# Splitting weight blocks four row tiles at a time, with two buffers instead of four

## The chip, the cores and the metric

The kernel runs on one core of one Trainium2 chip. The metric is the device time of one execution in microseconds (us); the figure to compare is the median of several runs. Five engines work side by side, each on its own queue of instructions in a fixed order: PE (TensorE, matrix products), DVE (VectorE), ACT (ScalarE), POOL (GpSimd) and SP, which here only issues DMAs. They wait for each other on semaphores.

## The reference

A decoder trunk of two pre-norm residual layers over 1024 tokens of width 1024, in float32. Each layer is a mixer with an input and an output projection, and a SwiGLU FFN of width 2816:

```
h = x
for layer in range(2):
    hn = rmsnorm(h, mix_norm_g[layer])
    # layer 0: causal pooling + Mamba-2 SSD; layer 1: RWKV-7 + RG-LRU
    h = h + mixer(hn @ w_in) @ w_out
    hn = rmsnorm(h, ffn_norm_g[layer])
    h = h + (silu(hn @ w_gate) * (hn @ w_up)) @ w_down
out = rmsnorm(h, final_norm_g)
```

## The kernel before

The 1024 tokens are worked in two halves of 512 (A and B), one half's mixer scan woven into the other's projections or FFN. A row tile is 128 rows of a weight, the contraction of one product.

To keep float32 accuracy with float32r products, each operand is split into a high half, which is its float32r rounding, and a low half, which is the rest. One product then takes three: high x high, high x low, low x high. Weights are split on chip. `wload` (L321) has SP load a block of four row tiles by 256 columns (512 KB) into one of three `raw` buffers. `wsplit` (L338) takes two row tiles at a time: an ACT cast writes `whi` (L348), then a DVE subtraction writes `wlo` (L349), both 128x512. `whi` and `wlo` each rotate through `BUFS["w"] = 4` buffers of two row tiles, that is two blocks. `dense` (L354) is the loop that uses them; it calls `wblock` for each block and then issues, for each row tile and each of two column tiles, the three products:

```
nc.tensor.matmul(o, wh[:, a:b], xh, start=st, stop=False)      # L370
nc.tensor.matmul(o, wh[:, a:b], xl, start=False, stop=False)   # L371
nc.tensor.matmul(o, wl[:, a:b], xh, start=False, stop=en)      # L372
```

So a block of four row tiles is 24 products of 128x512 on PE. Results are named by stage: `pi` (input projections), `po` (output projection), `pg` and `pu` (gate and up), `py` (down). The FFN goes over groups of column pairs, `GROUPS = (2, 2, 2, 2, 1, 1, 1)`: a group of two pairs has a down projection over four row tiles, a group of one pair over two row tiles, so that its "block" is half a block (L522 adds the result into `h`). The last group's down projection in the second layer (`ffn_final`) has buffers of its own (`alloc`, names `fh` and `fl`). `zload` (L326) loads blocks of 268 columns for z and dt, all eight row tiles of which are kept for four token chunks.

What else is named below: L236 and L302 write the low halves of normed activations, L304 and POOL's L300 the normed values themselves, L613 adds an output projection to the residual, L501 and L510 are the SwiGLU products. L861 makes the SSD's decays. In RWKV, L1166 are the products for the triangular blocks, L1169 masks them into `am`, L1172 and L1173 write `am` to DRAM and L1179 loads parts back in 16 small DMAs. L1040 and L1051 are RG-LRU's exponentials and roots on ACT.

The order of instructions on each engine is not written by hand: the program is emitted as in the loops above, and a scheduler (`schedule_with_timeline_sim=True`) then orders each engine's queue by its own model, and so settles which split, norm or scan instruction stands ahead of which.

Of the kernel before, what the change touches and what calls it, by code (L numbers as in the profile page):

```python
# [13 lines left out]
P = 128  # L14
D = 1024
S = 1024
# [10 lines left out]
BUFS = dict(h=8, m=28, act=5, raw=3, w=4, tf=3, sg=2, st=3, z=6,  # L27
# [64 lines left out]
class Trunk:  # L92
# [48 lines left out]
    def setup_params(self):  # L141
        nc, i = self.nc, self.i
        rows = [self.dp.tile([P, 512], F32, name=f"prow{k}", tag="tf", bufs=BUFS["tf"]) for k in range(2)]
        if NPARAM < 2 * P:
            nc.gpsimd.memset(rows[1], 0.0)
        r = 0
        for n, k in PARAM_ROWS:
            src = i[n]
            while len(src.shape) > 1:
                src = src.rearrange("a b -> (a b)") if len(src.shape) == 2 else src.rearrange("a b c -> (a b c)")  # L150
            src = src.rearrange("(r p) -> r p", p=P)
            done = 0
            while done < k:
                t, o = divmod(r, P)
                m = min(k - done, P - o)
                nc.gpsimd.dma_start(rows[t][o:o + m, :P], src[done:done + m, :])
                r += m
                done += m
        self.par = self.cp.tile([P, NPARAM], F32, name="par")
        ps = self.psum("ps_par")  # L160
        nc.tensor.transpose(ps[:, 0:P], rows[0][:, :P], self.c_ident)
        nc.tensor.transpose(ps[:, P:2 * P], rows[1][:, :P], self.c_ident)
        nc.scalar.copy(self.par, ps[:, :NPARAM])
        # derived parameters
        cw = self.cp.tile([P, 50], F32, name="cw")
        nc.vector.tensor_scalar(cw, self.par[:, PCOL["ssd_conv_w"]:PCOL["ssd_conv_w"] + 50], 0.5, None, op0=MULT)
        self.cw = cw
        omu = self.cp.tile([P, 14], F32, name="omu")
        nc.vector.tensor_scalar(omu, self.pv("rwkv_mu", 0, 14), -1.0, 1.0, op0=MULT, op1=ADD)
        self.omu = omu  # L170
        rkw = self.cp.tile([P, 4, 8], F32, name="rkw")
        nc.vector.tensor_tensor(rkw, self.c_ind.rearrange("p (j h) -> p j h", j=4),
                                self.pv("rwkv_r_k", 0, 4)[:, :, None].to_broadcast([P, 4, 8]), op=MULT)
        self.rkw = rkw
        # SSD per-head vectors on every partition
        hv = self.cp.tile([P, 3, 12], F32, name="hv")
        for k, n in enumerate(("ssd_dt_bias", "ssd_a_log", "ssd_d")):
            nc.gpsimd.dma_start(hv[:, k, :], i[n].broadcast_to([P, 12]))
        self.dtb, self.ssd_d = hv[:, 0, :], hv[:, 2, :]
        na = self.cp.tile([P, 12], F32, name="na")  # L180
        nc.scalar.activation(na, hv[:, 1, :], AF.Exp)
        nc.vector.tensor_scalar(na, na, -1.0, None, op0=MULT)
        self.nega = na
# [5 lines left out]
    def softplus(self, out, x, shape, pool, tag):  # L189
        """out = max(x, 0) + log1p(exp(-|x|)); log1p(u) = 2 atanh(u / (2 + u))."""  # L190
# [26 lines left out]
    def rsqrt1(self, y, x, t):  # L217
        """y = 1 / sqrt(x / 2^26) for [128, 1] operands; the factors that the steps leave cancel exactly."""
        nc = self.nc
        yi, xi = y.bitcast(I32), x.bitcast(I32)  # L220
        nc.vector.tensor_scalar(yi, xi, 1, None, op0=ALU.logical_shift_right)
        nc.vector.tensor_scalar(yi, yi, -1.0, float(0x5F3759DF - 2 ** 31), op0=MULT, op1=ADD)
        for c in (3.0, 12.0, 768.0):
            nc.vector.tensor_scalar(t, y, y, x, op0=MULT, op1=MULT)
            nc.vector.scalar_tensor_tensor(y, t, -c, y, op0=ADD, op1=MULT)

# [11 lines left out]
    def mm3(self, o, w, x, wr=slice(None), wc=slice(None), xr=slice(None)):  # L238
        """o = w^T x from the halves of w and x."""
# [42 lines left out]
    def hload(self, hf, k):  # L282
        """Residual tile k of a half from DRAM."""
        t = self.dp.tile([P, H], F32, name="hraw", tag="st", bufs=BUFS["st"])
        self.nc.sync.dma_start(t, self.hd[hf][k * P:(k + 1) * P, :])
        return t
# [4 lines left out]
    def norm_apply(self, out, h, r, gname, goff, hf=None):  # L291
        """Normalized and split tiles of a half appended to out; yields per tile."""
# [16 lines left out]
    def gain_apply(self, out, h, gname, goff):  # L309
        """Split tiles of h times the gain, whose 1 / rms their products still miss; yields per tile."""  # L310
# [15 lines left out]
    def zload(self, kk):  # L326
        """Rows kk * 128 .. of the first 256 columns of z and the 12 of dt."""
# [6 lines left out]
    def wblock(self, src, nk, width, alloc=None):  # L334
        """src: [nk*128, width] in DRAM -> list of (hi, lo) [128, <=2, width] tiles."""
        return self.wsplit(self.wload(src, nk, width), nk, width, alloc)

    def wsplit(self, raw, nk, width, alloc=None):  # L338
        nc = self.nc
        out = []  # L340
        for k in range(0, nk, 2):
            m = min(2, nk - k)
            if alloc:
                hi, lo = alloc()
            else:
                hi = self.dp.tile([P, 2, WB], F32R, name="whi", tag="whi", bufs=BUFS["w"])
                lo = self.dp.tile([P, 2, WB], F32R, name="wlo", tag="wlo", bufs=BUFS["w"])
# [6 lines left out]
    def dense(self, w, k0, nk, c0, width, rhs, ps, first=True, last=True):  # L354
        """ps[i] (<=128 columns of the weight each) += w[k0*128.., c0:c0+width]^T rhs; yields per block."""
# [25 lines left out]
    def load_x(self, hf, pool, tag, bufs):  # L381
        """x of a half, token-major, scaled by its rstd in place."""
# [24 lines left out]
    def start(self, pool, tag, bufs):  # L407
        """First half of x: norm and split chunk by chunk; the first weights of z run ahead of them."""
# [58 lines left out]
    def x_transposed(self, hf, k, pp):  # L467
        """Tiles k, k + 1 of x^T of a half into two PSUM banks, as the start of their accumulation."""
# [9 lines left out]
    def ffn(self, hf, layer, h, hn, nxt=None, r=None):  # L478
        """h updated in place; yields per weight block; returns Stat of the new h.
        nxt: the tiles that follow hn in its slots, emitted with the last products that read hn.  # L480
        r: 1 / rms per token where hn comes without it."""
# [66 lines left out]
    def ffn_final(self, hf, wd, base, act, h):  # L548
        """Last part of the last down projection, token-major, with the residual and the final norm."""
# [68 lines left out]
    # ================= even layer mixers =================  # L618
# [13 lines left out]
    def conv(self, hf, ps, w, b, car, out):  # L632
        """out = b + sum_k w[k] x[t - 3 + k], x in PSUM; w(k) -> [128, 1]; car: last 3 columns."""
# [10 lines left out]
    def in0(self, hf, hn, st, blk0=None):  # L644
        """Input projection of the even layer with what its columns need at once."""
# [34 lines left out]
    def in0_zdt(self, hf, hn, st, blk=None):  # L680
        """The first 256 columns of z and those of dt, token-major, a chunk after the other."""
# [127 lines left out]
    def ssd(self, hf, st):  # L809
        """SSD over the 4 chunks and 2 groups of a half; yields between steps."""  # L810
# [14 lines left out]
    def ssd_unit(self, hf, st, c, g):  # L825
# [10 lines left out]
        # token-major x and B  # L836
# [10 lines left out]
        # decay[s, h, t] = exp(min(cum_t - cum_s, 0)) for s <= t, for two chunks at a time  # L847
# [47 lines left out]
        # gate with silu(z), group RMS norm  # L895
# [20 lines left out]
    # ================= odd layer mixers =================  # L916
    def odd_open(self, pool):
# [12 lines left out]
        # softplus(-lambda)  # L930
# [13 lines left out]
    def shift(self, hf, ps, f, out):  # L944
        """out = p + mu (prev - p) for the tile f of the RWKV columns."""
# [15 lines left out]
    def in1(self, hf, hn):  # L961
# [24 lines left out]
        # RG-LRU: gate and branch  # L986
# [31 lines left out]
    def lru(self, hf, j2, xcs, ges):  # L1018
# [16 lines left out]
        for t in range(2):  # L1035
            # log_a = lam8 * rg; t = tanh(log_a / 2); 1 / (1 - t) = (1 + exp(log_a)) / 2 refined by one Newton step
# [8 lines left out]
            nc.vector.scalar_tensor_tensor(e, rg, 1.0, y, op0=ADD, op1=MULT)      # a  # L1045
            ys.append(y)
        for t in range(2):
# [4 lines left out]
            nc.vector.scalar_tensor_tensor(y, y, 2.0, rg, op0=MULT, op1=MULT)     # sqrt(1 - a^2)  # L1052
# [8 lines left out]
    def rwkv(self, hf, st):  # L1061
# [9 lines left out]
        # gates of decay and in-context rate  # L1071
# [5 lines left out]
        # squared norms of k * k_k, per head, token on partitions  # L1077
# [30 lines left out]
        # per chunk and head: [z; r] above [A_zk; A_rk]; the part of A that multiplies u  # L1108
# [49 lines left out]
        # inverses of the 32 x 32 diagonal blocks of I - A_zb, one instance per partition  # L1158
# [43 lines left out]
        def prep1(c):  # L1202
            """Token-major k|b and v of a chunk, and its A blocks."""
# [34 lines left out]
        def prep2(c):  # L1238
            """T^T = (I - A_zb)^-T: its diagonal blocks, and the first product of the other one."""
# [21 lines left out]
        def chain1(c):  # L1261
            """[G; Y'] = [z; r] S + [A_zk; A_rk] v"""
# [19 lines left out]
        def chain3(c):  # L1282
            """S <- e^{W_L} (S + [k; b]^T [v; u]), Y = Y' + A_rb u"""
# [48 lines left out]
    def gn(self, hf, c, y, v, bon, gd):  # L1332
        """Group norm, bonus and gate for 128 tokens, in two parts."""
# [49 lines left out]
class Side:  # L1383
    """Work emitted alongside a main stream."""
# [18 lines left out]
def weave(main, side, rate, limit=None):  # L1403
    """Emit main with rate steps of side after each of its steps, for limit steps at most."""
# [12 lines left out]
def hand(main, steps, nxt, side=None, rate=0, counts=(4, 4)):  # L1417
    """Emit main; the tiles nxt, that follow the operand of its last products, with the last two of its steps."""
# [121 lines left out]
```

## Time and profile before

| | us |
|---|---|
| Median of three runs (lowest, highest) | 2456.19 (2454.91, 2458.45) |
| Profiled execution, span from first to last instruction | 2456.8 |
| PE busy in it | 2424.1 |
| DVE, ACT, POOL busy | 1544.5, 915.7, 250.7 |
| `wlo` subtractions on DVE (744) | 539.4 |
| `whi` casts on ACT (744) | 459.2 |

The profiled execution's own time is known only as its span, 2456.8 us. Busy time is the union of an engine's instructions. PEld is the loading of the stationary operand, which overlaps the products. A row of the timeline has the start, the duration, the engine, the line, the operation, out<-in, shapes, a count and in brackets the idle time of the engine before it with what ended it.

### The profile page before, as it was taken

The numbers are of one execution on the slowest core, as the hardware profiler recorded it, in microseconds if no ns is written. First come the engines' busy times: TensorE is split into PE (matmuls) and PEld (weight loads), VectorE is DVE, ScalarE is ACT, GpSimd is POOL, SyncE is SP. The second block draws the span as 40 slices with busy tenths as digits, with TensorE's granted clock in tenths as the row PEclk, the third lists the DMA queues.
The fourth block names the chain that finished last, engine by engine and source line by source line (L and its number), as shares of the span: only waits on it lengthen the run. The fifth ranks groups of instructions, "written<-read, shape, count | busy, mean of one in ns | idle before, by whom it ended". The sixth has DMA issues, their size and how long they took to land.

```text
span 2456.8 us, 33271 instructions
## 1 busy us (share of the span) xinstructions
PE 2424.1 (99%) x12435; PEld 1982.7 (81%) x12435; DVE 1544.5 (63%) x3058; ACT 915.7 (37%) x1612; POOL 250.7 (10%) x235
## 2 busy tenths in 40 slices
PE   7999999999999999999999999999999999999998
PEld 6878888888878887788888888877888888888887
DVE  7888767764476675675565668576565547444445
ACT  4444343322244554233333346432333324222222
POOL 2131121211112010100000111020000001000000
PEclk9999999999999999999999999999999999999999
DMA  5223333233245332543324433234432433333322
GB/s 163 86 88 93 122 98 94 83 111 96 86 138 169 96 105 85 150 144 107 105 79 134 163 120 103 90 108 142 140 97 90 137 125 125 94 95 95 95 94 78
DMA packets 282513, 271.72 MB, mean 111 GB/s; under 512 B 45586, under 2 KB 260776, under 8 KB 282352
## 3 DMA queue, kind: packets, MB, share of 16 engines
q1 hardware_dynamic: 281520, 269.19, 35.4%
q8 instruction: 98, 1.61, 0.3%
q0 software_dynamic: 832, 0.41, 0.1%
q14 instruction: 63, 0.52, 0.1%
HBM read 239.14 MB, written 30.41 MB: 110 GB/s over the span
## 4 chain that ended last, share of the span: by engine, by line
PE 96%; DVE 2%; DMA 1%; issue 0%; ACT 0%; SPq 0%; DVEq 0%; ACTq 0%
PE pu L370 7%; PE pu L371 7%; PE pu L372 7%; PE pg L370 7%; PE pg L371 7%; PE pg L372 7%; PE py L370 6%; PE py L371 6%; PE py L372 6%; PE pi L370 5%; PE pi L372 5%; PE pi L371 5%; PE po L370 2%; PE po L371 2%; PE po L372 2%; PE ps_g L1269 1%
## 5 line engine op out<-in xcount | busy, mean ns | idle before, releaser
L349 DVE TENSOR_TENSOR wlo<-raw,whi 128x512 fp32r<-128x512 f32 (+1 forms) x744 | 539.4, 726 | 537.8 <-ACT whi L348 526.0
L348 ACT CAST whi<-raw 128x512 fp32r<-128x512 f32 (+1 forms) x744 | 459.2, 619 | 1093.3 <-PE pu L371 311.3
L370 PE MATMUL pu<-hnh,whi 128*128 128x512 f32 x736 | 293.9, 399 | 0.0
L371 PE MATMUL pu<-hnl,whi 128*128 128x512 f32 x736 | 292.8, 398 | 0.0
L372 PE MATMUL pu<-hnh,wlo 128*128 128x512 f32 x736 | 291.6, 396 | 0.0
L370 PE MATMUL pg<-hnh,whi 128*128 128x512 f32 x704 | 281.1, 399 | 0.0
L371 PE MATMUL pg<-hnl,whi 128*128 128x512 f32 x704 | 278.7, 396 | 0.0
L372 PE MATMUL pg<-hnh,wlo 128*128 128x512 f32 x704 | 277.2, 395 | 0.0
L371 PE MATMUL py<-actl,whi 128*128 128x512 f32 x672 | 267.2, 398 | 0.0
L370 PE MATMUL py<-acth,whi 128*128 128x512 f32 x672 | 263.6, 402 | 2.3 <-DVE sg L510 1.4
L372 PE MATMUL py<-acth,wlo 128*128 128x512 f32 x672 | 265.0, 396 | 0.0
L370 PE MATMUL pi<-hnh,whi 128*128 128x512 f32 x512 | 204.4, 400 | 1.8 <-DVE xbc L640 1.8
L371 PE MATMUL pi<-hnl,whi 128*128 128x512 f32 x512 | 204.2, 399 | 0.0
L372 PE MATMUL pi<-hnh,wlo 128*128 128x512 f32 x512 | 202.1, 397 | 0.0
L370 PEld LDWEIGHTS pu<-hnh,whi 128*128 128x128 f32 x736 | 138.7, 188 | 33.9 <-issue 2.2
L372 PEld LDWEIGHTS pu<-hnh,wlo 128*128 128x128 f32 x736 | 138.8, 189 | 32.9 <-issue 0.7
L371 PEld LDWEIGHTS pu<-hnl,whi 128*128 128x128 f32 x736 | 138.7, 188 | 32.2 <-issue 0.9
L370 PEld LDWEIGHTS pg<-hnh,whi 128*128 128x128 f32 x704 | 132.4, 188 | 31.1
L372 PEld LDWEIGHTS pg<-hnh,wlo 128*128 128x128 f32 x704 | 132.3, 188 | 30.8
L371 PEld LDWEIGHTS pg<-hnl,whi 128*128 128x128 f32 x704 | 132.3, 188 | 30.4
L370 PEld LDWEIGHTS py<-acth,whi 128*128 128x128 f32 x672 | 127.1, 189 | 34.2 <-ACT hnh L301 1.8
L372 PEld LDWEIGHTS py<-acth,wlo 128*128 128x128 f32 x672 | 127.0, 189 | 29.6
(451 smaller groups left out, 3766.1 us busy)
## 6 DMA issues: line engine op xcount, KB each, us to landing
raw<-in_ffn_w_gate SPq DMA_DIRECT2D x88, 512.0 KB
raw<-in_ffn_w_up SPq DMA_DIRECT2D x88, 512.0 KB
raw<-in_ffn_w_down SPq DMA_DIRECT2D x64, 512.0 KB
raw<-in_od_w_in SPq DMA_DIRECT2D x44, 512.0 KB
raw<-in_ev_w_in SPq DMA_DIRECT2D x36, 512.0 KB
raw<-in_ffn_w_down SPq DMA_DIRECT2D x48, 256.0 KB
yraw<-yd SPq DMA_DIRECT2D x32, 256.0 KB
raw<-in_ev_w_out SPq DMA_DIRECT2D x16, 512.0 KB
```

Of the source, the lines that this page charges most:

```text
L348: nc.scalar.copy(hi[:, :m, :width], raw[:, k:k + m, :width])
L349: nc.vector.tensor_tensor(lo[:, :m, :width], raw[:, k:k + m, :width], hi[:, :m, :width].bitcast(F32), op=SUB)
L370: nc.tensor.matmul(o, wh[:, a:b], xh, start=st, stop=False)
L371: nc.tensor.matmul(o, wh[:, a:b], xl, start=False, stop=False)
L372: nc.tensor.matmul(o, wl[:, a:b], xh, start=False, stop=en)
L1269: nc.tensor.matmul(pg[:, hs], e["w1"][:, h, :], e["S"][:, hs], start=h == 0, stop=h == 7)
```

## The change

`wsplit` takes four row tiles at a time where it allocates from the common pool, and `whi` and `wlo` have two buffers of four row tiles instead of four of two. The bytes of the buffers and the products stay the same; `ffn_final`'s splits stay at two row tiles. Comments and docstrings were taken out as well, and after `wsplit` the line numbers are one higher (L348 is L349, and so on).

```diff
-BUFS = dict(h=8, m=28, act=5, raw=3, w=4, tf=3, sg=2, st=3, z=6,
+BUFS = dict(h=8, m=28, act=5, raw=3, w=2, tf=3, sg=2, st=3, z=6,
...
     def wsplit(self, raw, nk, width, alloc=None):
         nc = self.nc
         out = []
-        for k in range(0, nk, 2):
-            m = min(2, nk - k)
+        step = 2 if alloc else 4
+        for k in range(0, nk, step):
+            m = min(step, nk - k)
             if alloc:
                 hi, lo = alloc()
             else:
-                hi = self.dp.tile([P, 2, WB], F32R, name="whi", tag="whi", bufs=BUFS["w"])
-                lo = self.dp.tile([P, 2, WB], F32R, name="wlo", tag="wlo", bufs=BUFS["w"])
+                hi = self.dp.tile([P, 4, WB], F32R, name="whi", tag="whi", bufs=BUFS["w"])
+                lo = self.dp.tile([P, 4, WB], F32R, name="wlo", tag="wlo", bufs=BUFS["w"])
             nc.scalar.copy(hi[:, :m, :width], raw[:, k:k + m, :width])
             nc.vector.tensor_tensor(lo[:, :m, :width], raw[:, k:k + m, :width], hi[:, :m, :width].bitcast(F32), op=SUB)
             for q in range(m):
                 out.append((hi[:, q, :], lo[:, q, :]))
```

The scheduler orders the new program anew. Three places show what moves. The first is DVE's queue in the odd layer's output projection of half A, where the norm of half B (`hn`, `hnl`) is emitted between its blocks. Before:

```order
L349 TENSOR_TENSOR wlo<-raw,whi 128x2x256
L236 TENSOR_TENSOR hnl_12619<-hn,hnh_12618 128x512
L304 SCALAR_TENSOR_TENSOR hn<-hraw,par,nrb 128x512
L302 SCALAR_TENSOR_TENSOR hnl_12627<-hn,par,hnh_12626 128x512
L349 TENSOR_TENSOR wlo<-raw,whi 128x2x256
L236 TENSOR_TENSOR hnl_12635<-hn,hnh_12634 128x512
L302 SCALAR_TENSOR_TENSOR hnl_12643<-hn,par,hnh_12642 128x512
L613 TENSOR_TENSOR h<-hraw,po 128x512 x2
L349 TENSOR_TENSOR wlo<-raw,whi 128x2x256 x2
```

After, at the same place:

```order
L350 TENSOR_TENSOR wlo<-raw,whi 128x4x256
L236 TENSOR_TENSOR hnl_11827<-hn,hnh_11826 128x512
L304 SCALAR_TENSOR_TENSOR hn<-hraw,par,nrb 128x512
L302 SCALAR_TENSOR_TENSOR hnl_11835<-hn,par,hnh_11834 128x512
L236 TENSOR_TENSOR hnl_11843<-hn,hnh_11842 128x512
L302 SCALAR_TENSOR_TENSOR hnl_11851<-hn,par,hnh_11850 128x512
L614 TENSOR_TENSOR h<-hraw,po 128x512 x2
L350 TENSOR_TENSOR wlo<-raw,whi 128x4x256
```

The split that stood between two norm operations, the last block's first half, is gone; the whole block is split where its second half was, behind both sums into h.

The second is PE's queue at the start of that same last block, `po` being its two accumulators. Before:

```order
L370 MATMUL po_12741<-yh_12379,whi_12783 128x512
L371 MATMUL po_12741<-yl_12380,whi_12783 128x512
L372 MATMUL po_12741<-yh_12379,wlo_12784 128x512
L370 MATMUL po_12742<-yh_12379,whi_12783 128x512
L371 MATMUL po_12742<-yl_12380,whi_12783 128x512
L372 MATMUL po_12742<-yh_12379,wlo_12784 128x512
```

After:

```order
L371 MATMUL po_11865<-yh_11603,whi_11903 128x512
L372 MATMUL po_11865<-yl_11604,whi_11903 128x512
L371 MATMUL po_11866<-yh_11603,whi_11903 128x512
L372 MATMUL po_11866<-yl_11604,whi_11903 128x512
L373 MATMUL po_11865<-yh_11603,wlo_11904 128x512
L373 MATMUL po_11866<-yh_11603,wlo_11904 128x512
```

The first use of wlo moved from the third product to the fifth.

The third is SP's queue in RWKV, half A, where `am` is written and parts of it loaded back (`A<-amd`), beside the FFN's weight loads. Before:

```order
L1173 DMA amd_8662<-am 64x1024
L1172 DMA w1d_8661<-am 64x1024
L1173 DMA amd_8662<-am 64x1024
L1179 DMA A<-amd_8662 8x32x32 x16
L323 DMA raw<-in_ffn_w_up 128x4x256
L323 DMA raw<-in_ffn_w_down 128x4x256 x4
```

After:

```order
L323 DMA raw<-in_ffn_w_up 128x4x256
L1173 DMA w1d_8101<-am 64x1024
L1174 DMA amd_8102<-am 64x1024
L1173 DMA w1d_8101<-am 64x1024
L1174 DMA amd_8102<-am 64x1024
L1180 DMA A<-amd_8102 8x32x32 x16
L323 DMA raw<-in_ffn_w_down 128x4x256 x4
```

The weight load that followed the 16 small loads now stands ahead of them and of the last writes of am.

## The prediction

> **What bounds the kernel now.** I read the page's totals and its chain first, then what TensorE (PE) waits for. Each row here names engine, busy time and share, or the wait, its total, its count and its longest.
>
> ```profile
> PE 2424.1 (99%) x12435; PEld 1982.7 (81%) x12435; DVE 1544.5 (63%) x3058; ACT 915.7 (37%) x1612; POOL 250.7 (10%) x235
> PE 96%; DVE 2%; DMA 1%; issue 0%; ACT 0%; SPq 0%; DVEq 0%; ACTq 0%
> PE ps_g L422 <- DMA grow<-in_mix_norm_g: 8.2, 1, 8.2
> PE ps_x L443 <- DVE xin L440: 4.6, 1, 4.6
> PE ps_A L1166 <- DVE am L1169: 3.0, 3, 2.2
> PE pi L370 <- DVE xbc L640: 1.8, 1, 1.8
> PE py L370 <- DVE sg L510: 1.4, 1, 1.4
> PE po L370 <- ACT hnh L235: 1.3, 1, 1.3
> PE po L370 <- ACT whi L348: 1.0, 1, 1.0
> PE py L370 <- DVE h L522: 0.8, 2, 0.6
> ```
>
> PE is the chain. After the start, whose two waits (8.2 and 4.6 us) are for inputs and the first norm, it waits 9.3 us in all for DVE and ACT (3.0 + 1.8 + 1.4 + 1.3 + 1.0 + 0.8). The splits cost 744 casts on ACT and 744 subtractions on DVE, but only 1.0 us of PE's waits is charged to them. So the change can win a few us at most; what matters is whether it makes PE wait.
>
> Is PE's 99% real? In the last projection stretch PE is without a gap, and one block's first product follows the last one's at once:
>
> ```profile
> 2060.00:2440.00 380.00, 380.00 (x1732) 311.52 (x1731) 176.74 (x305) 109.92 (x196) 0.00 (x0) 1.00 0.30 95
> 2087.16 0.40 PE L370 MATMUL pu<-hnh,whi 128*128 128x512 f32 x1
> 2092.74 0.39 PE L370 MATMUL pu<-hnh,whi 128*128 128x512 f32 x1
> 2092.71 0.62 ACT L348 CAST whi<-raw 128x512 fp32r<-128x512 f32 x1 [2.16 <-PE pu L371]
> 2093.36 0.69 DVE L349 TENSOR_TENSOR wlo<-raw,whi 128x512 fp32r<-128x512 f32 x1 [2.08 <-ACT whi L348]
> ```
>
> The first row holds window, PE, PEld, DVE, ACT, POOL, clock and DMA. The two matmuls are 24 products apart, one whole block: 5.58 us, 0.2325 each, half a block 2.79. The cast starts as its buffer comes free and the subtraction as the cast ends; cast and subtraction take 2094.05 - 2092.71 = 1.34 us.
> The Trainium skill ("Perfetto Trace Analysis", Identifying the Most-Contended Engine) holds that matmul busy time is no good measure of headroom and the weight-load share is. By it the 82% here (311.52 of 380) would leave a fifth to gain. The trace disagrees for feeding: with no gap between products, sooner operands gain nothing here.
>
> **What a split costs, and its lead.** Whole durations (minimum/median/maximum in ns), and other sizes for the slope:
>
> ```profile
> L348 ACT CAST whi<-raw x744: 602/621/642, 9.0 to 2421.7; 128x512 fp32r<-128x512 f32 x184, 128x536 fp32r<-128x536 f32 x2
> L349 DVE TENSOR_TENSOR wlo<-raw,whi x744: 659/691/1811, 9.6 to 2423.7; 128x512 fp32r<-128x512 f32 x184, 128x536 fp32r<-128x536 f32 x2
> L865 ACT ACTIVATE dec<-dec 128x384 f32<-128x384 f32 x32 | 16.1, 521 | 12.7 <-DVE dec L861 12.6
> L236 DVE TENSOR_TENSOR actl<-sg,acth 128x512 fp32r<-128x512 f32 x88 | 57.3, 683 | 0.1
> L873 DVE TENSOR_TENSOR dec<-dec,ps_cb 128x768 f32<-128x768 f32 x16 | 15.1, 946 | 4.0 <-PE ps_cb L872 4.0
> ```
>
> No 1024-wide split stands in the trace; from these rows I estimate ACT 0.621 + 512 x (0.621 - 0.521)/128 = 1.02 us, DVE 0.691 + 512 x (0.946 - 0.683)/256 = 1.22 us. The bounds are twice the 512 (1.24 and 1.38) and the 512 itself plus nothing, which the slope excludes. Of 744 splits 704 become 352; the 40 of two row tiles (down projections of single pairs) stay. ACT saves 352 x (1.24 - 1.02) = 77 us, DVE 352 x (1.38 - 1.22) = 56 us. Both engines run beside PE, so that alone is worth nothing.
>
> What the change takes is lead. With four half-size buffers, a split may start when the half block four back is read, three half blocks (3 x 2.79 = 8.37 us) before PE needs it: 8.37 - 1.34 = 7.0 us to spare. With two whole buffers it may start when the block two back is read, one block (5.58) before: the chain is 1.02 + 1.22 + 0.05 = 2.29, and 3.3 us remain. **In steady blocks that still costs 0.** For the two-tile splits the buffer ahead covers 2.79 against 1.34; two sums into h of 0.68 (as L236) may stand ahead on DVE: 1.34 + 1.36 = 2.70. That just fits: 0. Raw weights are freed 2.29 instead of 1.34 us after a block is read; a load takes 4.25 us (rows below, 1049.62 to 1053.87) and has 3 x 5.58 us: 0. SP's queue holds other DMAs behind that wait, but it already waits there 306 times:
>
> ```profile
> SPq L323 <- DVE wlo L349: 1354.5, 306, 10.8
> ```
>
> So the price is at places where ACT or DVE answers more than 3.3 us late. **First place: the odd layer's first output projection**, where the norm of the other half shares DVE, and DVE operations stretch to 1.79 us:
>
> ```profile
> 1414.49 1.78 DVE L349 TENSOR_TENSOR wlo<-raw,whi 128x512 fp32r<-128x512 f32 x1
> 1416.19 0.68 DVE L236 TENSOR_TENSOR hnl<-hn,hnh 128x512 fp32r<-128x512 f32 x1
> ...
> 1417.46 1.79 DVE L302 SCALAR_TENSOR_TENSOR hnl<-hn,par,hnh 128x512 fp32r<-128x512 f32 x1
> 1419.17 0.68 DVE L349 TENSOR_TENSOR wlo<-raw,whi 128x512 fp32r<-128x512 f32 x1
> 1422.09 1.27 DVE L613 TENSOR_TENSOR h<-hraw,po 128x512 f32<-128x512 f32 x2
> 1423.28 0.68 DVE L349 TENSOR_TENSOR wlo<-raw,whi 128x512 fp32r<-128x512 f32 x1
> 1421.71 0.39 PE L370 MATMUL po<-yh,whi 128*128 128x512 f32 x1
> ```
>
> The last block's halves are split at 1419.17 and 1423.28, ahead of their uses (1421.71 and 2.79 later). Now the one split stands where the second half stood, behind both h sums, while the first half's 0.6 us leave the queue: it ends at 1423.28 - 0.6 + 1.22 = 1423.9 at the earliest, 1424.1 with what is split sooner ahead of it. PE reads wlo first at 1421.71 + 0.93, since the new order puts four whi products ahead: 1422.64. **+1.4 us** (2.7 if nothing is saved ahead of it; 0 if DVE's queue is shorter there than I sum).
>
> **Second place: RWKV's triangular blocks, twice.** SP issues 16 small loads ahead of the weights:
>
> ```profile
> 1038.08 11.44 SPq L1179 DMA_DIRECT2D A<-amd  x16
> 1049.62 0.41 SPq L323 DMA_DIRECT2D raw<-in_ffn_w_up  x1
> 1053.87 1.14 ACT L348 CAST whi<-raw 128x512 fp32r<-128x512 f32 x2 [3.86 <-DMA raw<-in_ffn_w_up]
> 1055.46 0.39 PE L370 MATMUL pu<-hnh,whi 128*128 128x512 f32 x1
> ```
>
> With the old queue the merged split would end at 1053.87 + 2.29 = 1056.16, against 1055.46 + 0.46: 0.2 late, 0.9 with an activation product (L501, as long as L236) ahead on DVE. In the new order that load stands ahead of the 16, so it comes early; but if its buffer isn't free, the writes of am behind it wait, on which PE waited 3.0 us already. I take **+0.6** for both (0 to 1.8).
>
> **Third place: the even layer's first 330 us**, DVE at 81 to 85%. One split there, its cast done at 99.95, stood 6.0 us in DVE's queue:
>
> ```profile
> 35.00:110.00 75.00, 75.00 (x394) 62.51 (x392) 63.88 (x166) 36.98 (x70) 5.67 (x4) 1.00 0.31 92
> 185.00:275.00 90.00, 90.00 (x569) 79.32 (x568) 73.03 (x191) 37.05 (x71) 12.86 (x15) 0.98 0.30 91
> 99.33 0.62 ACT L348 CAST whi<-raw 128x512 fp32r<-128x512 f32 x1 [2.17 <-PE pz L725]
> 105.96 0.67 DVE L349 TENSOR_TENSOR wlo<-raw,whi 128x512 fp32r<-128x512 f32 x1
> 106.46 0.28 PE L724 MATMUL pz<-wlo,hnh 128*128 128x256 f32 x1
> ```
>
> If it kept that place, the merged one would end 0.53 later, at 107.16, 0.7 after PE's first use at 106.46. I allow three such waits, 2.1 us, an estimate since the new order shuffles DVE here: 0 to 3.5, taken **+1.5**.
>
> **The gain.** Each of the nine waits of 9.3 us follows a DVE or ACT queue; one merged split ahead of it saves 0.16 to 0.2 us: **-1.5**. Its bound is all 9.3.
>
> Sum: 0 + 1.4 + 0.6 + 1.5 - 1.5 = +2.0 us on the profiled 2456.8. That execution stands 0.6 us above the runs' median of 2456.19, and inside their range; on the median the forecast is 2458.2. A change of 0.2% (4.9 us) is about what can be told from none.
>
> **Rivals.**
> - Slower by lost lead: the scheduler's new orders cure nothing. Then the three places cost their upper ends, 2.7 + 1.8 + 3.5 = 8.0, and with 1.5 for each of two more crowded stretches of the odd input projections (ACT loads function tables there) 11 us: 2467. It decides once more than three places are over 1.5 us late. For it: lead falls from 7.0 to 3.3 everywhere. Against: one late block lets DVE catch up, so neighbours don't add.
> - Slower by the clock. Rows:
>
> ```profile
> 194.50:199.00 4.50, 4.50 (x14) 3.57 (x15) 2.53 (x10) 1.04 (x2) 0.83 (x1) 0.62 0.38 115
> 199.00:205.00 6.00, 6.00 (x27) 4.76 (x27) 3.53 (x6) 3.43 (x6) 0.00 (x0) 1.00 0.00 0
> 304.00:308.50 4.50, 4.50 (x13) 3.54 (x13) 1.55 (x5) 1.05 (x2) 0.00 (x0) 0.56 0.19 58
> ```
>
>   In 4.5 us 13 or 14 matmuls run instead of 19, at a granted 0.62 and 0.56: 1.3 us lost each. Five more such stretches on top of my sum give 2458.2 + 6.5 = 2465. The second stretch follows a place with PE waits of 1.0 and 1.3 us, the first follows none, so new waits of about 1 us may or may not call one.
>   The Trainium skill ("TensorE: Matmul & The Clock Gate", What's actually happening) says the clock halves after an idle window of about 3.4 us. By that rule my waits, none over 2.7 us, would call none.
> - Faster: the 133 us off ACT and DVE shorten most of PE's 9.3 us, and the reordered first 330 us lose their half-clock stretches (two, 2.6 us): up to 12, likely 7: 2449. Against: only 1.0 us of the waits is charged to a split.
> - The change does nothing visible (+0 to +1), since steady blocks hold 3.3 us of lead: it lies inside my forecast.
>
> **Chances.** Forecast (within 0.2%) 0.50; lost lead 0.28, clock 0.08, faster 0.14. So faster 0.14, same 0.50, slower 0.36. The likeliest case alone spans 2452 to 2461. The range for 8 in 10 reaches into both others: 2451 (leaving out most of the faster case, some 0.12) to 2470 (leaving out 0.06).
>
> **What would show it.** Casts near 1.02 us and subtractions near 1.22, 392 of each with fh's 8 apart; the same gapless PE from 2060 to 2440; new rows "PE ... <- DVE wlo" in PE's waits at 1417 to 1424 us, near 1056 and 1700, and before 330, each under 3 us. I am wrong if those rows sum to over 6 us, if a steady block waits (chain over 5.58), or if PE's waits for DVE shrink by more than 5.

## The result, and the profile after

| | before | after |
|---|---|---|
| Median of 20 runs each on one chip (lowest, highest), us | 2458.37 (2454.70, 2461.14) | 2461.26 (2458.65, 2462.53) |
| Ratio after to before, 95% interval | | 1.0013 [1.0007, 1.0019] |
| Profiled execution, span, us | 2456.8 | 2459.5 |

The kernel is 0.13% slower, some 3 us, inside the 0.2% that the forecast called no change. The forecast was +2.0 us. It came out near, but partly by luck: the odd layer lost more than I had put, and less time at half clock and two vanished waits in the even layer took most of it back.

Page of the kernel after, the totals and its chain:

```profile
PE 2422.6 (98%) x12435; PEld 1976.6 (80%) x12435; DVE 1502.6 (61%) x2706; ACT 852.8 (35%) x1260; POOL 251.8 (10%) x235
PE 89%; DVE 5%; DMA 2%; ACT 1%; SPq 1%; issue 1%; POOL 0%; DVEq 0%; ACTq 0%; POOLq 0%
```

DVE's busy time fell by 41.9 us and ACT's by 62.9, and the time did not fall: their busy time as such is not what the time is made of. PE's share of the chain went from 96 to 89% and DVE's from 2 to 5. The splits and one steady stretch:

```profile
L349 ACT CAST whi<-raw x392: 614/1048/1091, 8.8 to 2429.1; 128x1024 fp32r<-128x1024 f32 x174, 128x512 fp32r<-128x512 f32 x20, 128x1072 fp32r<-128x1072 f32 x2
L350 DVE TENSOR_TENSOR wlo<-raw,whi x392: 676/1225/2311, 9.9 to 2430.3; 128x1024 fp32r<-128x1024 f32 x174, 128x512 fp32r<-128x512 f32 x20, 128x1072 fp32r<-128x1072 f32 x2
2060.00:2440.00 380.00, 380.00 (x1727) 311.47 (x1726) 172.95 (x244) 100.33 (x137) 0.00 (x0) 1.00 0.34 101
```

A merged cast takes 1.05 us and a merged subtraction 1.23, and PE is as gapless from 2060 to 2440 us as before. What PE waited for (engine, operation, the releaser; sum in us, count, longest):

```profile
PE pi L371 <- DVE xbc L639: 2.4, 1, 2.4
PE py L373 <- DVE wlo L350: 2.0, 4, 0.7
PE ps_A L1167 <- DVE am L1170: 1.9, 2, 1.7
PE pi L371 <- DVE r L950: 1.6, 1, 1.6
PE po L373 <- DVE wlo L350: 1.5, 1, 1.5
PE py L371 <- DVE h L523: 1.3, 2, 1.0
PE pi L373 <- DVE wlo L350: 0.6, 1, 0.6
```

Three rows are new, waits for `wlo` of 4.1 us in all, and so is the wait for `r`. Two are gone: 1.0 for `whi` and 1.3 for `hnh` in the even layer's output projection. These rows do not say at what point the time was lost. For that I took each product by its names and shape, in its order, in both traces, and the median difference of the starts over 25 us. Where "after minus before" changes, time was lost or won:

| From to (us) | stage | difference at its end | change | forecast |
|---|---|---|---|---|
| 0-250 | even layer, input projections | +1.4 | +1.4 | +1.5 |
| 250-350 | its output projection, end of the SSD | -3.3 | -4.7 | -1.5 |
| 350-700 | its FFN, steady blocks | -3.6 | -0.3 | 0 |
| 700-1060 | to the first half's RWKV gates | -2.8 | +0.8 | 0 |
| 1060-1080 | triangular blocks, half A | -0.9 | +1.9 | +0.6 with half B |
| 1080-1415 | | -0.9 | 0 | 0 |
| 1415-1430 | odd layer's output projection | +0.9 | +1.8 | +1.4 |
| 1430-1550 | odd layer's input projections, half B | +3.4 | +2.5 | 0 |
| 1550-1700 | FFN, masks of half B | +1.7 | -1.7 | 0 |
| 1700-1730 | triangular blocks, half B | +3.6 | +1.9 | see half A |
| 1730-2440 | | +2.0 | -1.5 | 0 |

Three of these changes hold a difference of the clock. Before's profile has stretches at half the granted clock at 195, 301 and 1619 us, and the profile after has none there; each step of 3.41 us costs about 1.55 us (last section). Without these four steps the changes to 250, to 350 and to 1700 us would be about +2.9, -1.6 and -0.1, and the new kernel would end some 8 us behind instead of 2. The +0.8 at 700 to 1060 holds a new wait of 1.0 us for `h`, at 717 us.

An operation of known place bears the table out. `ps_kr` runs in RWKV's gates of each half; its first and last start stand behind the durations. Before, then after:

```profile
L1124 PE MATMUL ps_kr<-knT,indt_r x16: 387/392/500, 966.2 to 1617.8; 8*128 8x512 f32 x16
```

```profile
L1125 PE MATMUL ps_kr<-knT,indt_r x16: 384/392/506, 964.3 to 1621.9; 8*128 8x512 f32 x16
```

The new kernel reaches half A's gates 1.9 us earlier and half B's 4.1 us later.

### The profile page after: what moved, and what is told of

It is laid out like the page before. It is cut to its first block, busy times and chain, and to the rows that moved or that the text cites. A ratio compares the mean times of both kernels' runs of the same rounds, so it can differ in the third digit from the quotient of the medians.

```text
span 2459.5 us, 32078 instructions
## 1 busy us (share of the span) xinstructions
PE 2422.6 (98%) x12435; PEld 1976.6 (80%) x12435; DVE 1502.6 (61%) x2706; ACT 852.8 (35%) x1260; POOL 251.8 (10%) x235
## 4 chain that ended last, share of the span: by engine, by line
PE 89%; DVE 5%; DMA 2%; ACT 1%; SPq 1%; issue 1%; POOL 0%; DVEq 0%; ACTq 0%; POOLq 0%
PE pg L372 6%; PE pu L371 6%; PE pg L371 6%; PE pu L372 6%; PE pg L373 6%; PE pu L373 6%; PE py L371 6%; PE py L373 6%; PE py L372 6%; PE pi L371 4%; PE pi L373 4%; PE pi L372 4%; PE po L373 2%; PE po L371 2%; PE po L372 2%; PE ps_g L1270 1%
## 5 line engine op out<-in xcount | busy, mean ns | idle before, releaser
L349 ACT CAST whi<-raw 128x1024 fp32r<-128x1024 f32 (+2 forms) x392 | 393.7, 1004 | 978.8 <-PE pu L372 296.1
L350 DVE TENSOR_TENSOR wlo<-raw,whi 128x1024 fp32r<-128x1024 f32 (+2 forms) x392 | 465.9, 1188 | 322.2 <-ACT whi L349 311.5
L373 PE MATMUL pu<-hnh,wlo 128*128 128x512 f32 x736 | 283.4, 396 | 0.0
L373 PE MATMUL pg<-hnh,wlo 128*128 128x512 f32 x704 | 269.2, 395 | 0.0
L373 PE MATMUL py<-acth,wlo 128*128 128x512 f32 x672 | 253.6, 397 | 2.0 <-DVE wlo L350 2.0
L373 PE MATMUL pi<-hnh,wlo 128*128 128x512 f32 x512 | 196.1, 396 | 0.9 <-DVE wlo L350 0.6
L523 DVE TENSOR_TENSOR h<-h,py 128x512 f32<-128x512 f32 x160 | 108.1, 684 | 82.7 <-PE py L373 82.1
```

Of the source, the lines that this page charges most:

```text
L349: nc.scalar.copy(hi[:, :m, :width], raw[:, k:k + m, :width])
L350: nc.vector.tensor_tensor(lo[:, :m, :width], raw[:, k:k + m, :width], hi[:, :m, :width].bitcast(F32), op=SUB)
L523: nc.vector.tensor_tensor(h[f], h[f], pp[t], op=ADD)
```

## The experiments

Three theories stood against each other. Length: a subtraction of 1.2 us, whole or not at all, is late where DVE is crowded. Buffers: with two whole buffers a split may only start when a whole block has been read, so the lead is lost, whatever the operations' length. Order: each rebuild is ordered anew by the scheduler, and the time is a draw of some us.

### Length against buffers

The four share one set of runs; before had a median of 2457.92 us. **Halves in whole buffers** (`coarse_halves`): both operations work on two row tiles, in buffers of four.

```diff
-            nc.scalar.copy(hi[:, :m, :width], raw[:, k:k + m, :width])
-            nc.vector.tensor_tensor(lo[:, :m, :width], raw[:, k:k + m, :width], hi[:, :m, :width].bitcast(F32), op=SUB)
+            for j in range(0, m, 2):
+                e = min(m, j + 2)
+                nc.scalar.copy(hi[:, j:e, :width], raw[:, k + j:k + e, :width])
+                nc.vector.tensor_tensor(lo[:, j:e, :width], raw[:, k + j:k + e, :width], hi[:, j:e, :width].bitcast(F32), op=SUB)
```

> Two buffers of four row tiles as after, but each block cast and subtracted in two halves (128x512) as before. If it is the length of the merged subtraction that makes PE late (the first half of a block is ready 0.5 us later, and what stands behind the subtraction waits longer), the waits of PE for wlo, 4.1 us in the changed kernel, fall to about 1 us (the one at 1421 us to about 0.5), and the time is back at that of before, within 1.5 us. If it is the buffers (a buffer comes free only when the whole block is read), the waits for wlo stay at 3 to 5 us and the time at before +3. If it is the order that the scheduler happens to give, waits stand at other places and the time is anywhere within 4 us of before.

Measured: 2465.66 us, ratio 1.003 [1.0019, 1.004]. Waits for `wlo` 2.0 us (1.8 in the output projection, 0.2 else). Slowest of the four, with fewer such waits than the changed kernel: neither length nor buffers foretold that. The profiles tell a part: leaving out the last 10 us, `coarse_halves` stands at half clock for 20.5 us and the changed kernel for 6.8, which is worth some 6 us, and its last products stand 5.1 us behind those of the changed kernel. At equal clock, by this estimate, the two are about as fast: halving both operations won nothing back.

**One of the two merged**: in `cast_merged` only the subtraction is in the loop over `j`, in `sub_merged` only the cast.

> Buffers of four row tiles, the cast whole (128x1024), the subtraction in halves. DVE's queue is ordered at 1421 us as in the changed kernel, both sums into h ahead of the split. Length of the subtraction: the first half ends about 0.55 us after the split starts instead of 1.65, so the wait there falls from 1.5 to 0.4 to 0.6 us, waits for wlo sum to about 1 us, time before +0 to +1. Buffers: as the changed kernel, +3. Order: anywhere within 4 us.

> Buffers of four row tiles, the cast in halves, the subtraction whole. Length of the subtraction: waits for wlo 4 to 5 us as in the changed kernel (1.5 at 1421 us again), since the subtraction is as long and its second cast ends 0.2 us later; time before +3 to +4. Buffers: the same, +3. If ACT's saving mattered, this would be slower than the changed kernel by 1 us or more. Order: anywhere within 4 us.

Measured: `cast_merged` 2457.62, ratio 0.9997 [0.9988, 1.0006]; `sub_merged` 2459.18, ratio 1.0004 [0.9995, 1.0012]. The waits for `wlo` in `cast_merged`:

```profile
PE po L375 <- DVE wlo L352: 1.1, 1, 1.1
PE pu L375 <- DVE wlo L352: 0.6, 2, 0.4
PE py L375 <- DVE wlo L352: 0.4, 2, 0.2
```

They are 2.1 us against 4.1 in the changed kernel and 5.2 in `sub_merged`. So in this pair the length of the subtraction goes with about half of the waits, and the other half stays with halves in whole buffers. At 1421 us I had expected 0.4 to 0.6 and 1.1 stayed: there most of the wait stays with the buffers. The times of the two overlap. `cast_merged` stands at half clock for 6.8 us like the changed kernel, and its last products stand 4.0 us ahead of that kernel's; why `coarse_halves`, with the same halved subtraction, wins nothing stays open.

**Low products last** (`low_last`): more lead with the same splits.

```diff
+            for q in range(n):
+                wl, xh = blk[q][1], rhs[kk + q][0]
+                for t in range(nt):
+                    a, b = t * P, min(width, (t + 1) * P)
+                    en = last and kk + q == nk - 1
+                    nc.tensor.matmul(ps[t][:b - a, :], wl[:, a:b], xh, start=False, stop=en)
```

and the third product of the inner loop is gone.

> The changed kernel with one more edit: the eight products that read wlo come last in each block instead of each behind its two whi products. PE then asks for wlo 16 products, 3.7 us, after a block's start instead of 0.5, and whi comes free 1.9 us before the block's end, so the lead of a split grows from 3.3 to about 7 us at the same sizes and buffers. If lost lead (by length or by buffers) is the cause, PE's waits for wlo vanish (under 0.5 us in all) and the time is at before or below, by 0 to 2 us. If only the order decides, it is anywhere within 4 us, with waits for other things.

Measured: 2457.53, ratio 0.9999 [0.999, 1.0008]. Its waits for `wlo` are 0.2 us in all, as lead foretold, but others took their place:

```profile
PE pi L370 <- DVE xbc L645: 4.8, 1, 4.8
PE py L370 <- DVE sg L515: 2.9, 2, 1.5
PE pi L370 <- DVE r L954: 2.5, 1, 2.5
```

So the waits for `wlo` follow the lead, and the time does not follow the waits for `wlo` alone. Here, too, the profile has 20.5 us at half clock.

### Which layer

The layers have pools of their own (`ep`, `op`). With the buffers moved from the common pool into these, each layer's size can be chosen by itself. With the same sizes, DVE, ACT, PE and SP keep their orders but for some 10 to 20 rows (`halves_moved` against before, `whole_moved` against after):

```diff
-        step = 2 if alloc else 4
+        odd = hasattr(self, "op")
+        pool, size = (self.op, 2) if odd else (self.ep, 4)
+        step = 2 if alloc else size
...
-                hi = self.dp.tile([P, 4, WB], F32R, name="whi", tag="whi", bufs=BUFS["w"])
-                lo = self.dp.tile([P, 4, WB], F32R, name="wlo", tag="wlo", bufs=BUFS["w"])
+                hi = pool.tile([P, size, WB], F32R, name="whi", tag="whi", bufs=8 // size)
+                lo = pool.tile([P, size, WB], F32R, name="wlo", tag="wlo", bufs=8 // size)
...
         with tc.tile_pool(name="ep", bufs=1) as ep:
+            t.ep = ep
```

This is `even_merged`; the three others have other pairs of 2 and 4. Before had 2456.24 us in these runs.

> The kernel before with its buffers of halves in each layer's own pool, a control for the two others: the queues are the same but for some 10 to 20 rows where the layers meet. 0, within 1.5 us, in either theory. Its profile is also a second one of the old order: if the stretches at half clock are fixed by the order, they stand again at 195, 301, 977, 1619 and 1670 us; if by chance, at other places.

> Whole splits in two buffers of four row tiles in the even layer, halves in four buffers of two in the odd layer; the buffers lie in each layer's own pool. Against the kernel before, the changed kernel stood 2.4 us ahead in the profiles at 975 us, the end of the even layer, and 2.0 behind at the end. If the change gains in the even layer and loses in the odd one, this kernel shows the gain alone: before -2 to -4 us, no wait for wlo near 1063, 1421, 1494 or 1711 us. If each order that the scheduler gives is a draw of its own, it is anywhere within 4 us of before.

> The opposite: halves in the even layer, whole splits in the odd layer. If the loss is in the odd layer, this kernel shows it alone: before +4 to +7 us, with waits for wlo near 1063, 1421, 1494 and 1711 us of 4 to 5 us in all, and PE's waits near 282 and 298 us as before. As a draw of its own: anywhere within 4 us of before, and the two kernels' differences need not sum to the changed kernel's +3.

> The changed kernel with its buffers in each layer's own pool: before +3, within 1.5 us, in either theory, and the control for the changed kernel. If the half-clock stretches follow the order, two again (at 976 and 1673 us) and none at 301; if chance, other places. Waits for wlo sum to 4 us again.

| | median, us | ratio to before, 95% interval | against `halves_moved`, us |
|---|---|---|---|
| `halves_moved` (2, 2) | 2459.86 | 1.0017 [1.0008, 1.0025] | |
| `even_merged` (4, 2) | 2458.90 | 1.0011 [1.0003, 1.002] | -1.0 |
| `odd_merged` (2, 4) | 2468.39 | 1.0046 [1.0033, 1.0059] | +8.5 |
| `whole_moved` (4, 4) | 2466.57 | 1.0042 [1.003, 1.0054] | +6.7 |

The control missed its 0: the move itself costs 3.6 us, for PE now waits where the layers meet, 3.3 us by the row

```profile
PE pi L373 <- POOL S L1269: 3.3, 1, 3.3
```

So all are read against it; `whole_moved`, expected at +3, is at +10.3 against before, which the move and the +6.7 make up. The parts add up (-1.0 + 8.5 = 7.5 against 6.7 for both), which a draw for each kernel as a whole would not do. The starts of the products show the places. From 800 us, where the layers have met, to the end, `odd_merged` falls back by 4.7 us against `halves_moved` and `whole_moved` by 8.3, though both have fewer stretches at half clock there than the control: **the loss is in the odd layer**. In the even layer `even_merged` is 0.7 us behind at 800 us; the gain of 2 to 4 us that I had expected of it is not there (its -1.0 is not told from 0). The size of the +8.5 is less sure than it looks: in the profiles `odd_merged` is 11.3 us behind, and 5.0 of these arise ahead of 750 us, where it splits in halves as the control does (a longer wait at 283 us, and a stretch at half clock at 301 us that the control has not). And the sums do not tell lead from order: an order drawn once for each layer would add up as well.

`odd_merged`'s largest wait is where the layers meet, as in the control, now for the first merged split (first row). It has three of the odd layer's waits again, at the same places:

```profile
PE pi L373 <- ACT whi L351: 3.7, 1, 3.7
PE py L375 <- DVE wlo L352: 2.0, 4, 0.7
PE pi L373 <- DVE r L952: 1.3, 1, 1.3
PE pi L375 <- DVE wlo L352: 0.5, 1, 0.5
```

At the place of the 1421 us it has none. There its split stands behind both sums into `h` too, but it takes 1.21 us and not 1.65, and ends before PE asks for it (1430.98):

```profile
1429.66 1.21 DVE L352 TENSOR_TENSOR wlo<-raw,whi 128x1024 fp32r<-128x1024 f32 x1
```

A profile is also very exact where the order is the same. From 1050 us to the end, one order for both, `even_merged` runs 1.85 to 1.92 us behind `halves_moved`.

### Lead alone

In these runs before had 2459.77 us. First the kernel before with fewer buffers and nothing merged (`w=3` and `w=2` in `BUFS`, one number each):

> The kernel before (halves) with three buffers of two row tiles instead of four, nothing merged. A split may start two half blocks before PE needs it: 5.58 - 1.34 = 4.2 us of lead, near the changed kernel's 3.3. If the buffers' lead is what the changed kernel loses, waits for wlo of 1.5 to 3 us in all appear near 1063, 1421, 1494 and 1711 us, and the time is before +1 to +3. If the length of the merged operations is it, 0 within 1.5 us and no such waits.

> The kernel before with two buffers of two row tiles: 2.79 - 1.34 = 1.45 us of lead. Lead: now also steady blocks wait where two operations of 0.68 stand ahead on DVE; before +10 to +60 us, with waits for wlo by the dozen. Length of the operations: the chain of 1.34 us still fits into a half block of 2.79, so within 2 us of before.

Then a pair whose sources differ in one number only. To make room for a third whole buffer, other buffers are given up in both:

```diff
-BUFS = dict(h=8, m=28, act=5, raw=3, w=2, tf=3, sg=2, st=3, z=6,
+BUFS = dict(h=8, m=28, act=5, raw=2, w=3, tf=2, sg=2, st=2, z=6,
```

and `w=2` in the control.

> Control for the next: the changed kernel with two raw buffers instead of three and two instead of three of the tiles st (residual rows) and tf (scratch), which makes room for a third buffer of each half. Fewer buffers can only add waits: before +3 to +12 us, waits for wlo 4 us or more.

> As the control, but three whole buffers of whi and of wlo: the lead grows from 3.3 to 11.16 - 2.29 = 8.9 us at the same merged operations. If lost lead is the cause of the odd layer's waits, those for wlo fall under 0.5 us in all and the time is 2 to 5 us under the control's. If the length of the merged subtraction is the cause (it stands in DVE's queue for 1.2 us whatever the buffers), the waits stay within 1 us of the control's and so does the time.

| | median, us | ratio to before, 95% interval |
|---|---|---|
| `halves_3buf` | 2449.87 | 0.9963 [0.9951, 0.9976] |
| `halves_2buf` | 2470.97 | 1.0043 [1.003, 1.0056] |
| `whole_2buf_tight` | 2471.92 | 1.0052 [1.004, 1.0065] |
| `whole_3buf_tight` | 2461.37 | 1.0009 [1.0, 1.0018] |

The pair is the test of the theory. The control's waits for a split:

```profile
PE pi L373 <- DVE wlo L350: 3.8, 4, 1.5
PE po L371 <- ACT whi L349: 2.9, 1, 2.9
PE py L373 <- DVE wlo L350: 2.2, 5, 0.7
PE pu L371 <- ACT whi L349: 1.4, 2, 0.8
PE py L371 <- ACT whi L349: 0.8, 1, 0.8
```

These 11.1 us are all gone with the third buffer: no row for `wlo` or `whi` is left, at the same merged operations, and the time falls by 10.6 us, more than the 2 to 5 expected. Both profiles have 10.2 us at half clock ahead of the last 10 us, so the clock is not the difference. The order is not the same in the two (by operands and shapes 88 of SP's 763 rows, 220 of DVE's 2706 and up to a third of PE's products stand elsewhere), and the kernel with three buffers has waits that the other has not, 3.9 us for `hnl` at 788 to 800 us. But not one wait for a split is left: **lost lead is what makes PE wait for a merged split**, and its length alone is not enough. `halves_2buf` says the same from the other side: halves with little lead wait 8.4 us for `wlo` in six rows and cost 11.2 us, with no stretch at half clock ahead of the last 10 us, where before has 20.5.

`halves_3buf` missed: with less lead than before I expected +1 to +3 us and it is 9.9 us faster, and beats both kernels of this case. Its waits for `wlo` are there as expected (0.9 and 0.4 us), but others are gone:

```profile
PE pu L372 <- DVE wlo L349: 0.9, 1, 0.9
PE ps_A L1166 <- DVE am L1169: 0.6, 1, 0.6
PE po L372 <- DVE wlo L349: 0.4, 1, 0.4
```

Before, `ps_A` waited 3.0 us for `am`, and the rows for `whi`, `hnh` and `sg` held 3.7 more. The larger part is the clock: 6.8 us at half clock in this profile against 20.5 in before's, worth some 6 of the 9.1 us by which its last products stand ahead. The other runs say the same: the mean granted clock was 0.997 to 0.999 in the five of `halves_3buf` and 0.994 to 0.996 in the 15 of before.

One of the waits can be followed further. The DMAs that SP issues and the mask on DVE, half B, first before, then `halves_3buf`:

```profile
1660.24 0.55 SPq L323 DMA_DIRECT2D raw<-in_ffn_w_up  x1
1660.88 0.47 SPq L1172 DMA_DIRECT2D w1d<-am  x1
1661.40 0.59 SPq L1173 DMA_DIRECT2D amd<-am  x1
1667.58 1.29 DVE L1169 TENSOR_TENSOR am<-ps_A,cst 128x512 f32<-128x512 f32 x2 [5.54 <-DMA amd<-am]
```

```profile
1654.92 0.56 SPq L1172 DMA_DIRECT2D w1d<-am  x1
1655.54 0.59 SPq L1173 DMA_DIRECT2D amd<-am  x1
1659.34 1.29 DVE L1169 TENSOR_TENSOR am<-ps_A,cst 128x512 f32<-128x512 f32 x2 [3.25 <-DMA amd<-am]
1661.83 0.57 SPq L323 DMA_DIRECT2D raw<-in_ffn_w_up  x1
```

Before, a weight load of 512 KB is issued just ahead of the writes of `am`, and DVE stands idle 5.54 us until a buffer of `am` is written out. In `halves_3buf` the load is issued 6.3 us behind the write, and DVE's idle time is 3.25. The 2.3 us between are as much as PE's wait of 2.2 at this `ps_A` before, which is gone (the 0.6 that is left stands at 1024 us). That the load ahead is the cause is read from the order of these rows; no run moved this load alone. Why this rebuild came out well at several such places, and whether fewer buffers as such make it so, stays open.

## Why the prediction was right

**Steady blocks, 0: right.** From 350 to 700 us the difference goes from -3.3 to -3.6 us: with half the lead nothing is lost there.

**The price of a split: right.** 1.05 and 1.23 us against my 1.02 and 1.22. The splits' own busy time fell by 65.5 us on ACT (459.2 to 393.7) and 73.5 on DVE (539.4 to 465.9), against my 77 and 56. The time did not follow.

**The output projection, +1.4: right in place and size, with other parts.** The wait is 1.5 us, the change of difference 1.8:

```profile
1419.25 5.21 POOL L262 TENSOR_TENSOR nacc<-nacc,nsq 128x512 f32<-128x512 f32 x3 [1.36 <-ACT nsq L260]
1420.40 1.35 DVE L614 TENSOR_TENSOR h<-hraw,po 128x512 f32<-128x512 f32 x2 [0.69 <-DMA hraw<-hd]
1421.66 1.65 DVE L350 TENSOR_TENSOR wlo<-raw,whi 128x1024 fp32r<-128x1024 f32 x1
1423.37 0.73 PE L373 MATMUL po<-yh,wlo 128*128 128x512 f32 x2 [1.49 <-DVE wlo L350]
```

The split stands behind both sums into `h`, as the order had told. But my sum had neither the sums' own wait of 0.69 us for `hraw` nor the 1.65 us of the split, instead of 1.22, beside POOL's sums. `odd_merged`, whose split stands behind both sums too and has neither of the two, has no wait there: the queue's order alone did not make the 1.5.

**RWKV's blocks, +0.6 (0 to 1.8): mis-sized, and at the wrong product.** They cost 1.9 us each, of which waits for `wlo` hold 1.0, and not at `pu` near 1056 but in the down projection behind it:

```profile
1068.75 0.40 PE L372 MATMUL py<-actl,whi 128*128 128x512 f32 x1
1069.23 1.05 ACT L349 CAST whi<-raw 128x1024 fp32r<-128x1024 f32 x1 [6.06 <-PE py L372]
1069.87 0.68 DVE L523 TENSOR_TENSOR h<-h,py 128x512 f32<-128x512 f32 x1
1070.79 0.68 DVE L523 TENSOR_TENSOR h<-h,py 128x512 f32<-128x512 f32 x1
1071.72 1.22 DVE L350 TENSOR_TENSOR wlo<-raw,whi 128x1024 fp32r<-128x1024 f32 x1
1072.99 0.73 PE L373 MATMUL py<-acth,wlo 128*128 128x512 f32 x2 [0.72 <-DVE wlo L350]
```

The step that failed is "it may start when the block two back is read, one block (5.58) before". That holds where blocks are read one after the other. Here PE's order takes the products of two blocks in turns from 1061.7 us on, since the activations of the second pair come late, and the older one's last product with `whi` is the first row: 1068.75. PE asks for the low half of the block two on at 1072.27 (1072.99 - 0.72), 3.1 us after that product's end and not 5.58. The chain from there took 3.8 us to 1072.94, since both sums into `h` and steps of the scan stood ahead of the subtraction on DVE.

**The even layer's first 330 us, +1.5: right in size, wrong in cause.** The difference is +1.4 at 250 us, but not one wait for `wlo` stands there. The wait for `xbc` grew from 1.8 to 2.4 us; the rest was not traced. And it is +1.4 only since before has a stretch at half clock at 195 us, worth about 1.5 us.

**The gain, -1.5 (bound -9.3): mis-sized.** The waits at 282 and 298 us are gone, and with them a stretch of 6.8 us at half clock; 4.7 us in all. Merging is not needed for that: `halves_3buf` loses the same waits with nothing merged, and `halves_moved`, with halves in before's order, has them shorter (0.3 and 0.9 us against 1.0 and 1.3), has no stretch at 301 us and stands some 4 us ahead of before from 300 to 750 us. So the gain was mostly luck of the execution and not the change's.

**What I had not put in the sum: the input projections of half B, +2.5.** The rival of lost lead named this place, at 1.5 for each of two stretches. The first is a wait for `wlo` at 1495; the second is ACT's queue:

```profile
1507.48 1.05 ACT L349 CAST whi<-raw 128x1024 fp32r<-128x1024 f32 x1 [3.19 <-PE pi L372]
1512.29 1.28 ACT L1041 ACT_TABLE_LOAD   x1
1514.83 1.24 ACT L949 ACTIVATE r<-pi,omu 128x512 f32<-128x512 f32 x2
1516.34 0.50 PE L371 MATMUL pi<-hnh,whi 128*128 128x512 f32 x1 [1.56 <-DVE r L950]
```

The cast stands at the head of ACT's queue until its whole buffer comes free, and all behind it, table loads and the emptying of PE's own accumulators, starts later. Before, a cast of a half stood there too and waited 3.16 us, but it started at 1503.84; the merged one starts 3.6 us later, where PE's products run only 2.0 us later. PE then waits for its accumulator and not for a split. A split that waits can thus cost more than its own row shows.

So the forecast held its bound because two errors met, which is luck: the odd layer lost 8.1 us at its four places (1.9 + 1.8 + 2.5 + 1.9, of which my terms held 2.0), and the half-clock time (some 6 us) and two waits of the even layer took it back. The rival of lost lead was right about the odd layer; that of the clock was wrong in sign: after has 6.8 us at half clock ahead of the last 10 us, before had 20.5.

## What to carry to other kernels

Merging two operations off the path is worth nothing by the time that it saves there; ask what the coarser buffer does to the time between "free again" and "needed", in the order in which the matrix engine really reads, and what stands in the queue behind an operation that waits for it. Where a scheduler orders the program anew, hold a change of a few us against a control with the same order (here the buffers moved into the layers' pools), and compare the time at half clock, since a rebuild can move the time by several us (`halves_3buf` won 9.9 with more waits for `wlo` than before, most of it by the clock). And before giving loads more lead, look at whose DMA they are issued ahead of; this last is read from rows and was not tested.

## What the runs showed of the hardware that I had not expected

The half-clock stretches start on a fixed grid. Windows of the kernel before (window, length, busy PE, PEld, DVE, ACT and POOL with counts, granted clock, DMA):

```profile
195.30:198.71 3.41, 3.41 (x9) 2.66 (x9) 1.73 (x7) 1.00 (x2) 0.31 (x1) 0.50 0.32 112
297.70:301.11 3.41, 2.13 (x12) 1.42 (x10) 2.03 (x7) 2.37 (x5) 0.85 (x1) 1.00 0.27 103
301.11:307.94 6.83, 6.83 (x24) 5.86 (x23) 4.44 (x13) 1.84 (x4) 0.83 (x1) 0.50 0.24 76
```

In all 13 profiles that have more than one such stretch (`halves_2buf` has only its last), they start a whole number of steps of 3.4133 us from each other, and last one or two of these, but for the last, in which the kernel ends (before: 195.30, 301.11, 976.95, 1618.66 and 1669.86, that is 31, 198, 188 and 15 steps apart). The grid's place differs from profile to profile. Cut along it, a window in which PE was busy for under 45% was followed by a half-clock window in 17 of 18 cases; 45 to 70%, in 10 of 44; 70 to 80%, in 2 of 47; 80 to 99%, in none of 223. The middle row above is one: busy 2.13 of 3.41 us, then 6.83 us at 0.50.
Of 9593 windows without a wait 20 were followed by one too, three of them already at half clock; the other 17 held 9 or more products of `ps_seg` (12 rows of the array; 4 of 50 such windows) or 4 or more of `ps_kr` (8 rows; 13 of 26). So what counts seems to be how much of the array works, not idleness alone. The same wait of 2.37 us near 175 us called a stretch in `even_merged` and none in the kernel after, and `halves_moved`, with before's order, has before's stretches at 195, 1619 and 1670 us again but not those at 301 and 977: where the grid lies decides, too.

In such a stretch the products of 128x512 start 0.43 us apart and not 0.23 (before, four of them from 1619.91 to 1621.19), so a step of 3.41 us costs 3.41 x (1 - 0.2325/0.4267) = 1.55 us, a little under half. Across before's stretch at 1619 us, which the kernel after has not, the difference of the starts goes from +3.25 to +1.69.
The Trainium skill ("TensorE: Matmul & The Clock Gate", What's actually happening) gives this window, 4096 cycles or 3413 ns, running freely. The length and the free phase agree with these traces. Its idle window doesn't: 1.3 us of waits in a window (3.41 - 2.13) was enough at 298 us. By that rule I had expected my waits to call no stretch; the 13.7 us between the two kernels' half-clock time are worth some 6.2 us, more than the whole difference in question.

DVE's subtractions lengthen only beside POOL's operations, and not always. In the kernel after, the 309 of 128x1024 that no POOL operation overlaps last 1229 ns at most; of the 39 that one overlaps, 11 last over 1350 ns, up to 2311 beside a norm at 1413 us, and 1.65 us at 1421 beside POOL's sums. Before, of the 128x512 subtractions none of 655 lasts over 695 ns without POOL, and 39 of 81 last 823 to 1811 ns beside it.
